# Gate products of 512 columns: the input's rounded part and remainder side by side

## The chip, the cores and the metric

The kernel runs on one core of a Trainium2 chip. The metric is the device time of one execution in microseconds (us), the median of several. A core has TensorE (PE in the profile, its weight loads PEld), VectorE (DVE), ScalarE (ACT), GpSimd (POOL), and SyncE (SP), which issues most DMAs. Each of DVE, ACT and POOL works through its instructions in the order of the program; where one engine needs another's result it waits on a semaphore.

## The reference

Two layers of a decoder trunk over 256 positions of 1024 channels. Each layer mixes tokens by three branches (latent attention A, dilated window attention B, attention over selected keys C) and then runs a mixture of 32 experts. The change concerns the gates of the branches:

```python
o_a = mla_branch(...); o_b = dilated_branch(...); o_c = dsa_branch(...)
g = jax.nn.sigmoid(x @ w_gate + b_gate).reshape(B, S, 3, D)
merged = g[:, :, 0] * (o_a @ w_a) + g[:, :, 1] * (o_b @ w_b) + g[:, :, 2] * (o_c @ w_c)
return merged @ w_o
```

`x @ w_gate` is a product of 256 × 1024 by 1024 × 3072, in float32.

## The kernel before

Float32 products of the mixer are made of three products in a faster format (fp32r). `split` (L357) cuts a float32 tile in two: ACT rounds it (L361), and DVE, at the start of a layer now and then POOL, takes the remainder (L362). `mm3` (L364) then adds rounded × rounded, rounded × remainder and remainder × rounded in PSUM (L366, L367, L368).

A layer's input, transposed, lies in two tiles of 8 × 256 columns: `xTh`, its rounded part, and `xTl`, its remainder. They are made by `make_xT` in layer 0 and by `next_T` and `next_split` in layer 1. The mixer's weights come in as a stream of DMAs into a ring of 26 slots (1 MB each). They are worked off in a fixed list of pieces, built by `pieces` (L557): first the input projection, then for each branch gates and output projections by turns, then the common output projection. A piece has `prep`, which splits 1024 columns of its weights into a slot `ws`, and `prod`, its products in two parts. `mixer` (L1326) runs part 0 and part 1 of a piece, and calls `prep` of a piece five ahead behind part 1 (four ahead near the end). After each part it pops steps of the three branches' attention from queues, by due times and estimated delays: scores, reductions (L870), exponentials (L880), division (L892), transposes (L905), products with the values (L918), top-k (L1072, L1073), the selection mask (L1082 to L1085). All that is decided when the program is built; on the chip each engine keeps to that order.

A gate piece makes one tile of 128 gate channels × 256 positions: 8 k, each with `mm3` of 256 columns, into half of a PSUM bank. There are 24 such pieces a layer, 48 in all. Behind the last product ACT runs Tanh out of the bank (L647; a sigmoid by way of tanh, its bias and scale in the instruction). `merge` (L739) multiplies the gate later with the branch's projection: L744 for branch A, L747 for B and C. PSUM has eight banks, taken in turn (`bank`). Small tiles of the tag `t1` share five buffers. `evac` (L348) copies out of PSUM on ACT or DVE, whichever has the smaller sum of estimated costs so far; `note` adds to these sums.

Of the kernel before, what the change touches and what calls it, by code (L numbers as in the profile page):

```python
# [10 lines left out]
F32 = mybir.dt.float32  # L11
F32R = mybir.dt.float32r
BF = mybir.dt.bfloat16
I32 = mybir.dt.int32
AF = mybir.ActivationFunctionType
ALU = mybir.AluOpType
# [3 lines left out]
P = 128  # L20
L = 2
T = 256
NT = 2
D = 1024
KD = 8
# [23 lines left out]
T1 = 5  # L49
# [261 lines left out]
class Trunk:  # L311
# [52 lines left out]
    def mm3(self, out, sh, sl, mh, ml, start, stop):  # L364
# [2 lines left out]
        m(out, sh, ml, start=False, stop=False)  # L367
        m(out, sl, mh, start=False, stop=stop)  # L368

    def warm(self, n, src):  # L370

        ps = self.bank()
        for _ in range(n):
            self.nc.tensor.matmul(ps, src[:, 0:P], src[:, 0:512], start=True, stop=True)
# [162 lines left out]
    def make_xT(self, t):  # L537
        nc = self.nc
        if t == 0:
            self.xTh = self.slots.alloc([P, KD, T], F32R, "xTh")  # L540
            self.xTl = self.slots.alloc([P, KD, T], F32R, "xTl")
        ts = slice(t * P, (t + 1) * P)
        for k in range(0, KD, 4):
            ps = self.bank()
            for j in range(4):
                nc.tensor.transpose(ps[:, j * P:(j + 1) * P], self.x[:, t, (k + j) * P:(k + j + 1) * P], self.ident)
            self.split(self.xTh[:, k:k + 4, ts], self.xTl[:, k:k + 4, ts], ps.rearrange("p (k t) -> p k t", k=4), 512)

    def wsplit(self, src, n, shape):
        w = self.slots.alloc([P, 2, n], F32R, "ws")  # L550
# [6 lines left out]
    def pieces(self, l):  # L557

        out = []

        def win(c):
            name, c0, w = CHUNKS[c]
            st = {}
            nk = 2 if w > 256 else 4
            np_ = KD // nk
            for i in range(np_):
                h, kk = (i // 2, i % 2) if w > 256 else (0, i)

                def prep(h=h, kk=kk):
                    raw = self.ring.get((l, "in", c, h))  # L570
                    return self.wsplit(raw[:, kk * nk:(kk + 1) * nk, :], nk * w, (P, nk, w))

                def prod(sp, part, i=i):
                    if "ps" not in st:
                        st["ps"] = [self.bank() for _ in range(NT)]
                    for t in (part,):
                        for j in range(nk):
                            k = i * nk + j
                            ts = slice(t * P, (t + 1) * P)
                            self.mm3(st["ps"][t][:, :w], self.xTh[:, k, ts], self.xTl[:, k, ts], sp[1][:, j], sp[2][:, j],  # L580
                                     k == 0, k == KD - 1)
                    if i == np_ - 1:
                        self.put_pj(st["ps"][part], part, c0, w)
                        if part:
                            self.mark(("in", c))

                last = (l, "in", c, h) if (w <= 256 and i == np_ - 1) or (w > 256 and kk == 1) else None
                out.append((prep, prod, last, None))
# [37 lines left out]
        def gates(br, q):  # L626

            for j in range(2):
                ct = q * 2 + j

                def prep(j=j):
                    raw = self.ring.get((l, "gate", br, q))
                    return self.wsplit(raw[:, :, j * P:(j + 1) * P], 1024, (P, 8, P))

                def prod(sp, part, ct=ct, st=None):
                    if part == 0:
                        self.gps = self.bank()
                    ps = self.gps
                    for k in range(part * 4, part * 4 + 4):
                        self.mm3(ps[:, :T], sp[1][:, k], sp[2][:, k], self.xTh[:, k], self.xTl[:, k], k == 0, k == KD - 1)  # L640
                    if part == 0:
                        return
                    gp = self.slots.part("g", 8)
                    g = gp.ap
                    b = br * 8 + ct
                    self.note("act", T)
                    self.nc.scalar.activation(g, ps[:, :T], AF.Tanh, bias=self.hbg[:, b:b + 1], scale=0.5)  # L647
                    self.g[br, ct] = gp
                    if br == 2 and ct == 7:
                        self.slots.free(self.xTh, self.xTl)  # L650

                out.append((prep, prod, (l, "gate", br, q) if j else None, None))

# [878 lines left out]
    def next_T(self, t):  # L1532

        nc = self.nc
        if t == 0:
            self.xTh = self.slots.alloc([P, KD, T], F32R, "xTh")
            self.xTl = self.slots.alloc([P, KD, T], F32R, "xTl")
            self.xps, self.xy = {}, {}
        xps = self.xps[t] = [self.bank() for _ in range(4)]
        for k in range(KD):  # L1540
            nc.tensor.transpose(xps[k // 2][:, k % 2 * P:(k % 2 + 1) * P], self.x[:, t, k * P:(k + 1) * P], self.ident)
# [14 lines left out]
    def next_split(self, t, h):  # L1556
        ts = slice(t * P, (t + 1) * P)
        for j in range(2):
            k = 4 * h + 2 * j
            self.split(self.xTh[:, k:k + 2, ts], self.xTl[:, k:k + 2, ts], self.xy[t, h][j], 256)  # L1560

    def ln2_out(self, t, acc, c, pool):

# [434 lines left out]
```

## Time and profile before

| | us |
|---|---|
| median of 3 runs | 982.09 (981.78 to 984.99) |
| the profiled execution | 979.94 |
| its span, first to last instruction | 978.1 |
| TensorE busy | 902.0 (92%) |
| DVE busy | 467.0 (48%) |
| ACT busy | 415.6 (42%) |
| POOL busy | 147.9 (15%) |

The first mixer takes the span up to about 290 us, the first layer's experts up to about 494, the second mixer up to about 772, the second layer's experts and the last normalisation the rest. The gates of layer 0 have their Tanh between 143.8 and about 253 us, those of layer 1 between about 626 and 736.

In the profile's timelines a row has a start, a time and an engine, then the line, the operation, the tiles (out<-in) and shapes, and the count of instructions that the row merges; brackets tell how long the engine was idle before it and what ended that. A matmul's time is longer than the distance to the next one, since matmuls overlap: its pace is read from starts.

### The profile page before, as it was taken

The numbers are of one execution on the slowest core, as the hardware profiler recorded it, in microseconds if no ns is written. First come the engines' busy times: TensorE is split into PE (matmuls) and PEld (weight loads), VectorE is DVE, ScalarE is ACT, GpSimd is POOL, SyncE is SP. The second block draws the span as 40 slices with busy tenths as digits, with TensorE's granted clock in tenths as the row PEclk, the third lists the DMA queues.
The fourth block names the chain that finished last, engine by engine and source line by source line (L and its number), as shares of the span: only waits on it lengthen the run. The fifth ranks groups of instructions, "written<-read, shape, count | busy, mean of one in ns | idle before, by whom it ended". The sixth has DMA issues, their size and how long they took to land.

```text
span 978.1 us, 18621 instructions
## 1 busy us (share of the span) xinstructions
PE 902.0 (92%) x7626; PEld 706.2 (72%) x7627; DVE 467.0 (48%) x968; ACT 415.6 (42%) x911; POOL 147.9 (15%) x246
## 2 busy tenths in 40 slices
PE   8999999999999995799889999999999999775994
PEld 7988899999995652455379888998999855441541
DVE  6848677845563110110388686677556521101104
ACT  6545556644553230222274646666345524210221
POOL 2531110012100000000035071100271000000002
PEclk9999999999999997789999999999999999986997
DMA  9933161396889999999993033415849899999993
GB/s 373 384 127 129 44 259 44 140 376 218 309 318 360 421 421 419 420 420 420 420 422 138 27 130 129 174 53 217 351 162 423 314 407 420 421 420 420 420 420 160
DMA packets 41421, 284.85 MB, mean 291 GB/s; under 512 B 4850, under 2 KB 5618, under 8 KB 9074
## 3 DMA queue, kind: packets, MB, share of 16 engines
q1 hardware_dynamic: 41044, 283.38, 72.5%
q8 instruction: 62, 1.02, 0.4%
q10 hardware_dynamic: 288, 0.23, 0.1%
q14 instruction: 27, 0.22, 0.1%
HBM read 282.55 MB, written 1.05 MB: 290 GB/s over the span
## 4 chain that ended last, share of the span: by engine, by line
PE 61%; DMA 30%; POOL 3%; DVE 2%; issue 2%; ACT 1%; SPq 0%; POOLq 0%; ACTq 0%; DVEq 0%
DMA w<-in_stream_dram 28%; PE bank L366 13%; PE bank L367 13%; PE bank L368 13%; PE bank L1730 4%; PE bank L864 3%; PE bank L1684 2%; PE bank L918 2%; PE bank L905 2%; DMA gb<-in_ln_dram 2%; PE bank L1809 2%; PE bank L867 1%; POOL t L773 1%; PE bank L485 1%; PE bank L1487 1%
## 5 line engine op out<-in xcount | busy, mean ns | idle before, releaser
L362 DVE TENSOR_TENSOR ws<-w,ws 128x1024 fp32r<-128x1024 f32 (+2 forms) x154 | 188.8, 1235 | 127.5 <-ACT ws L361 123.6
L361 ACT ACTIVATE ws<-w 128x1024 fp32r<-128x1024 f32 (+2 forms) x158 | 158.5, 1022 | 31.9 <-PE bank L368 14.4
L1730 PE MATMUL bank<-w,xg 128*32 128x256 f32 x2048 | 134.0, 401 | 31.8 <-DMA w<-in_stream_dram 24.1
L1730 PEld LDWEIGHTS bank<-w,xg 128*32 128x32 f32 x2048 | 66.5, 115 | 102.3 <-DMA w<-in_stream_dram 29.7
L366 PE MATMUL bank<-ws,xTh 128*128 128x408 f32 (+3 forms) x320 | 115.4, 361 | 1.2 <-ACT xTh L361 1.2
L366 PE MATMUL bank<-xTh,ws 128*128 128x256 f32 x384 | 111.2, 290 | 0.0
L367 PE MATMUL bank<-ws,xTh 128*128 128x408 f32 (+3 forms) x320 | 109.3, 342 | 1.2 <-POOL ws L362 1.2
L368 PE MATMUL bank<-ws,xTl 128*128 128x408 f32 (+3 forms) x320 | 109.6, 342 | 0.7 <-DVE xTl L362 0.7
L367 PE MATMUL bank<-xTl,ws 128*128 128x256 f32 x384 | 108.6, 283 | 0.0
L368 PE MATMUL bank<-xTh,ws 128*128 128x256 f32 x384 | 108.5, 283 | 0.0
L1688 ACT ACTIVATE xg<-bank,gpk 128x128 f32<-128x128 f32 x128 | 51.6, 453 | 99.6 <-PE bank L1684 96.4
L1758 DVE SCALAR_TENSOR_TENSOR t<-t,cw,bank 128x256 f32<-128x256 f32 x16 | 7.7, 480 | 156.2 <-PE bank L1730 156.2
L366 PEld LDWEIGHTS bank<-xTh,ws 128*128 128x128 f32 x384 | 73.5, 191 | 1.8 <-issue 1.0
L367 PEld LDWEIGHTS bank<-xTl,ws 128*128 128x128 f32 x384 | 73.6, 192 | 0.2
L368 PEld LDWEIGHTS bank<-xTh,ws 128*128 128x128 f32 x384 | 73.5, 191 | 0.0
L880 ACT ACTIVATE p<-bank,nb 128x128 f32<-128x128 f32 (+1 forms) x92 | 37.2, 419 | 69.9 <-DVE nb L872 62.3
L366 PEld LDWEIGHTS bank<-ws,xTh 128*128 128x128 f32 x320 | 60.5, 189 | 7.7 <-issue 1.7
L1809 PE MATMUL bank<-w,t 128*32 128x512 f32 (+1 forms) x544 | 61.8, 571 | 2.6 <-DMA w<-in_stream_dram 1.4
L368 PEld LDWEIGHTS bank<-ws,xTl 128*128 128x128 f32 x320 | 60.4, 189 | 5.3 <-DVE xTl L362 1.0
L367 PEld LDWEIGHTS bank<-ws,xTh 128*128 128x128 f32 x320 | 60.6, 189 | 4.6 <-POOL ws L362 1.5
L1684 PEld LDWEIGHTS bank<-xg,x 128*128 128x128 f32 x512 | 60.4, 192 | 3.5 <-issue 2.5
L1684 PE MATMUL bank<-xg,x 128*128 128x128 f32 x512 | 62.4, 276 | 0.0
(343 smaller groups left out, 1523.8 us busy)
## 6 DMA issues: line engine op xcount, KB each, us to landing
w<-in_stream_dram SPq DMA_DIRECT2D x252, 1024.0 KB, 13.4
w<-in_stream_dram SPq DMA_DIRECT2D x12, 816.0 KB, 14.8
w<-in_stream_dram SPq DMA_DIRECT2D x4, 832.0 KB, 8.4
w<-in_stream_dram SPq DMA_DIRECT2D x2, 768.0 KB, 12.3
x<-in_x_dram SPq DMA_DIRECT2D x2, 512.0 KB, 4.1
w<-in_stream_dram SPq DMA_DIRECT2D x2, 512.0 KB, 15.0
out_dram<-x SPq DMA_DIRECT2D x4, 256.0 KB, 2.2
masks<-in_masks_dram SPq DMA_DIRECT2D x1, 512.0 KB, 11.4
```

Of the source, the lines that this page charges most:

```text
L361: self.nc.scalar.activation(hi, src, AF.Copy)
L362: (self.nc.gpsimd if self.lo_pool else self.nc.vector).tensor_tensor(lo, src, hi.bitcast(F32), op=ALU.subtract)
L366: m(out, sh, mh, start=start, stop=False)
L367: m(out, sh, ml, start=False, stop=False)
L368: m(out, sl, mh, start=False, stop=stop)
L864: nc.tensor.matmul(b[:, j * w:(j + 1) * w], q[:, blk * P:(blk + 1) * P], k[:, 0:w], start=j == 0, stop=False)
L880: nc.scalar.activation(p[:, j], v[:, j], AF.Exp, bias=nb[:, j:j + 1], scale=u["scale"], accum_out=sm[:, j:j + 1])
L905: nc.tensor.transpose(ps[:, n * P:(n + 1) * P], p[:, j * P:(j + 1) * P], self.ident)
L1684: nc.tensor.matmul(ps[:, i * P:(i + 1) * P], self.xn[:, t, k + i], pm[:, t, j:j + Q].rearrange("p e c -> p (e c)"), start=t == 0, stop=t = ...
L1688: nc.scalar.activation(xg[:, k + i], ps[:, i * P:(i + 1) * P], AF.Identity, bias=b, scale=g)
L1730: nc.tensor.matmul(hp[i * CAP:(i + 1) * CAP, c * 256:(c + 1) * 256], xg[:, k, i * CAP:(i + 1) * CAP], w[i], start=k == 0, stop=k == KD - 1 ...
L1809: nc.tensor.matmul(yp[q * CAP:(q + 1) * CAP, :w], hT[:, j, q * CAP:(q + 1) * CAP], w2[q][:, j], start=j == 0, stop=j == 1, tile_position=( ...
```

## The change

The gates' product takes the input's rounded part and its remainder as one moving operand of 512 columns. A new `mm2` makes, for each k, one product of the rounded weights with both (512 columns, a whole bank) and one of the weights' remainder with the rounded input (256 columns, the first half). The order of the two is turned round after the first k. For that the two tiles of x are laid out anew: each of two tiles holds four k, and for each the rounded 256 columns and the 256 of the remainder side by side. Behind the last product ACT copies the second half of the bank to a `t1` tile, DVE adds the first half to it, and ACT runs Tanh on the sum. The input projection's products stay as they were, with operands from the new tiles. The estimates get one more cost on ACT and one on DVE for each gate.

```diff
+    def mm2(self, out, sh, sl, mv, start, stop):
+
+        m = self.nc.tensor.matmul
+        n = T
+        if not start:
+            m(out[:, :n], sl, mv[:, 0], start=False, stop=False)
+        m(out, sh, mv, start=start, stop=stop)
+        if start:
+            m(out[:, :n], sl, mv[:, 0], start=False, stop=False)
...
     def make_xT(self, t):
         nc = self.nc
         if t == 0:
-            self.xTh = self.slots.alloc([P, KD, T], F32R, "xTh")
-            self.xTl = self.slots.alloc([P, KD, T], F32R, "xTl")
+            self.xT = [self.slots.alloc([P, 4, 2, T], F32R, "xT") for _ in range(2)]
...
-            self.split(self.xTh[:, k:k + 4, ts], self.xTl[:, k:k + 4, ts], ps.rearrange("p (k t) -> p k t", k=4), 512)
+            self.split(*(self.xT[k // 4][:, :, j, ts] for j in range(2)), ps.rearrange("p (k t) -> p k t", k=4), 512)
...
                     for k in range(part * 4, part * 4 + 4):
-                        self.mm3(ps[:, :T], sp[1][:, k], sp[2][:, k], self.xTh[:, k], self.xTl[:, k], k == 0, k == KD - 1)
+                        self.mm2(ps, sp[1][:, k], sp[2][:, k], self.xT[k // 4][:, k % 4], k == 0, k == KD - 1)
                     if part == 0:
                         return
                     gp = self.slots.part("g", 8)
                     g = gp.ap
                     b = br * 8 + ct
                     self.note("act", T)
-                    self.nc.scalar.activation(g, ps[:, :T], AF.Tanh, bias=self.hbg[:, b:b + 1], scale=0.5)
+                    s = self.t([P, T], F32, "t1", T1)
+                    self.note("dve", T)
+                    self.note("act", T)
+                    self.nc.scalar.activation(s, ps[:, T:], AF.Copy)
+                    self.nc.vector.tensor_tensor(s, s, ps[:, :T], op=ALU.add)
+                    self.nc.scalar.activation(g, s, AF.Tanh, bias=self.hbg[:, b:b + 1], scale=0.5)
                     self.g[br, ct] = gp
...
     def next_split(self, t, h):
         ts = slice(t * P, (t + 1) * P)
         for j in range(2):
-            k = 4 * h + 2 * j
-            self.split(self.xTh[:, k:k + 2, ts], self.xTl[:, k:k + 2, ts], self.xy[t, h][j], 256)
+            self.split(*(self.xT[h][:, 2 * j:2 * j + 2, i, ts] for i in range(2)), self.xy[t, h][j], 256)
```

## Rows read from the trace of the kernel before

**Rows 1.** The page: busy time of the engines, and the chain that ended last.

```profile
PE 902.0 (92%) x7626; PEld 706.2 (72%) x7627; DVE 467.0 (48%) x968; ACT 415.6 (42%) x911; POOL 147.9 (15%) x246
...
PE 61%; DMA 30%; POOL 3%; DVE 2%; issue 2%; ACT 1%; SPq 0%; POOLq 0%; ACTq 0%; DVEq 0%
```

**Rows 2.** Busy us of each engine by stretch, granted clock, DMA share, GB/s.

```profile
136.00:150.00 14.00, 14.00 (x125) 13.57 (x124) 10.11 (x21) 9.77 (x22) 0.00 (x0) 1.00 0.25 85
150.00:170.00 20.00, 20.00 (x165) 18.43 (x164) 13.38 (x31) 11.14 (x40) 0.00 (x0) 1.00 0.14 49
170.00:190.00 20.00, 20.00 (x176) 18.65 (x176) 17.74 (x40) 11.86 (x24) 0.00 (x0) 1.00 0.44 163
...
230.00:250.00 20.00, 20.00 (x169) 20.00 (x168) 9.14 (x13) 9.46 (x15) 2.91 (x4) 1.00 0.52 183
...
318.00:445.00 127.00, 105.86 (x1110) 62.54 (x1111) 16.74 (x34) 27.55 (x69) 5.50 (x9) 0.89 1.01 420
...
660.00:680.00 20.00, 20.00 (x185) 18.08 (x184) 16.44 (x31) 11.69 (x26) 0.00 (x0) 1.00 0.54 205
```

**Rows 3.** Timeline of PE: 17 products of 512 columns, 46 of 256, first and last.

```profile
111.83 0.39 PE L367 MATMUL bank<-ws,xTh 128*128 128x512 f32 x1
...
115.49 0.39 PE L368 MATMUL bank<-ws,xTl 128*128 128x512 f32 x1
...
136.03 0.28 PE L368 MATMUL bank<-xTh,ws 128*128 128x256 f32 x1
...
141.42 0.28 PE L368 MATMUL bank<-xTh,ws 128*128 128x256 f32 x1
```

**Rows 4.** Line 647 as a whole, then ACT's timeline around gates of either layer.

```profile
L647 ACT ACTIVATE g<-bank,hbg x48: 452/473/521, 143.8 to 736.3; 128x256 f32<-128x256 f32 x48
...
136.84 0.66 ACT L352 ACTIVATE vB<-bank 128x256 f32<-128x256 f32 x2
...
143.77 0.49 ACT L647 ACTIVATE g<-bank,hbg 128x256 f32<-128x256 f32 x1
144.13 1.08 ACT L361 ACTIVATE ws<-w 128x1024 fp32r<-128x1024 f32 x1
145.08 0.49 ACT L647 ACTIVATE g<-bank,hbg 128x256 f32<-128x256 f32 x1
145.43 1.08 ACT L361 ACTIVATE ws<-w 128x1024 fp32r<-128x1024 f32 x1
...
679.55 0.47 ACT L647 ACTIVATE g<-bank,hbg 128x256 f32<-128x256 f32 x1 [1.24 <-PE bank L368]
```

**Rows 5.** DVE's timeline: the remainders of the first gates' pieces, a merge.

```profile
145.24 2.53 DVE L362 TENSOR_TENSOR ws<-w,ws 128x1024 fp32r<-128x1024 f32 x2 [2.58 <-ACT ws L361]
...
157.89 0.41 DVE L744 SCALAR_TENSOR_TENSOR merged<-g,bank 128x256 f32<-128x256 f32 x1
```

**Rows 6.** Timelines of three engines: what attention's products need, and when they run.

```profile
148.16 1.13 ACT L352 ACTIVATE qkT<-bank 128x512 f32<-128x512 f32 x2
...
153.19 0.71 PE L864 MATMUL bank<-qkT 64*128 64x128 f32 x8
...
161.00 0.23 DVE L1085 TENSOR_SCALAR cs<-cs 128x128 bf16<-128x128 f32 x1
...
162.56 0.60 PE L867 MATMUL bank<-cs,mk 128*128 128x512 bf16 x2
...
176.88 0.69 DVE L892 TENSOR_TENSOR p<-p,r 128x512 f32<-128x512 f32 x1
...
177.39 1.04 PE L905 MATMUL bank<-cst,p 128*128 128x128 f32 x8
```

**Rows 7.** PE's timeline: branch B's output is waited for, layer 0, layer 1.

```profile
205.32 0.39 PE L366 MATMUL bank<-oTB,ws 128*128 128x256 f32 x1 [0.48 <-ACT oTB L361]
...
687.30 0.39 PE L366 MATMUL bank<-oTB,ws 128*128 128x256 f32 x1 [0.48 <-ACT oTB L361]
```

**Rows 8.** Timelines: a late gate on ACT, the output projection's remainders on DVE, their use.

```profile
233.08 0.47 ACT L647 ACTIVATE g<-bank,hbg 128x256 f32<-128x256 f32 x1 [2.41 <-PE bank L368]
...
264.34 2.36 DVE L362 TENSOR_TENSOR ws<-w,ws 128x1024 fp32r<-128x1024 f32 x2 [1.44 <-ACT ws L361]
...
267.21 0.39 PE L367 MATMUL bank<-ws,mT 128*128 128x512 f32 x1
```

More of the change, by code (lines that the diff above doesn't have):

```diff
@@ L571, in prep, with prod @@
                     return self.wsplit(raw[:, kk * nk:(kk + 1) * nk, :], nk * w, (P, nk, w))
-                def prod(sp, part, i=i):
+                def prod(sp, part, n=i):
                     if "ps" not in st:
@@ L577, in prod @@
                         for j in range(nk):
-                            k = i * nk + j
+                            k = n * nk + j
                             ts = slice(t * P, (t + 1) * P)
-                            self.mm3(st["ps"][t][:, :w], self.xTh[:, k, ts], self.xTl[:, k, ts], sp[1][:, j], sp[2][:, j],
+                            self.mm3(st["ps"][t][:, :w], *(self.xT[k // 4][:, k % 4, i, ts] for i in range(2)), sp[1][:, j], sp[2][:, j],
                                      k == 0, k == KD - 1)
-                    if i == np_ - 1:
+                    if n == np_ - 1:
                         self.put_pj(st["ps"][part], part, c0, w)
@@ L646, in prod @@
                     self.note("act", T)
-                    self.nc.scalar.activation(g, ps[:, :T], AF.Tanh, bias=self.hbg[:, b:b + 1], scale=0.5)
+                    s = self.t([P, T], F32, "t1", T1)
[4 more added lines that the diff above has]
+                    self.nc.scalar.activation(g, s, AF.Tanh, bias=self.hbg[:, b:b + 1], scale=0.5)
                     self.g[br, ct] = gp
                     if br == 2 and ct == 7:
-                        self.slots.free(self.xTh, self.xTl)
+                        self.slots.free(*self.xT)
                 out.append((prep, prod, (l, "gate", br, q) if j else None, None))
@@ L1535, in next_T @@
         if t == 0:
-            self.xTh = self.slots.alloc([P, KD, T], F32R, "xTh")
-            self.xTl = self.slots.alloc([P, KD, T], F32R, "xTl")
+            self.xT = [self.slots.alloc([P, 4, 2, T], F32R, "xT") for _ in range(2)]
             self.xps, self.xy = {}, {}
```

## The prediction

> **What bounds the kernel now.** I read the page first [rows 1]: TensorE is busy 92% of the span, and the chain that ended last lies on it for 61%, on DMAs for 30%. By stage [rows 2] these are two kinds of stretch. In both mixers (the rows from 136 to 250 and from 660 us) the matmul row is full, the clock is whole and the DMA engines are 14% to 54% busy: TensorE bounds, and nothing hides time added to or taken from its queue. From 318 us the DMA engines are saturated and TensorE waits for experts' weights. All gates lie in the mixers, 24 to a layer, so what the change does there moves all that follows: the stream of experts' weights is let in by slots that the mixer frees, and moves with it.
>
> The engines beside TensorE come next. Over 230 to 250 us ACT and DVE are busy 47% and 46%; over 170 to 190 us DVE is busy 89% and ACT 59%, over 660 to 680 us 82% and 58% [rows 2]. So the two halves of the gates differ: in the first half of each layer attention runs in between, in the second it doesn't. What matters is how far ACT and DVE run behind TensorE, and what TensorE takes from them: that I read from the three engines' timelines.
>
> **TensorE's part.** For each of 8 k the change puts one product of 512 columns and one of 256 where three of 256 stood. In a gate of now, 45 products of 256 follow one another from 136.03 to 141.42 us: 0.1198 us each [rows 3]. In the input projection 16 products of 512 take from 111.83 to 115.49: 0.2288 us each [rows 3]. So a k costs 0.3594 us now and 0.3486 after: 0.0108 us saved, 0.086 a gate, 4.1 us over 48 gates × 8. The weight load that goes isn't counted by itself: it lies under the matmul before it. The two paces make a fixed 0.0108 us a product, beside 0.1090 for 256 columns. That a 256 keeps its pace between two 512s no row shows; the saving lies between none and, if it loses its fixed part too, 8 us. I take 4.1, the nearest to the rows.
>
> The Trainium skill (TensorE: Matmul & The Clock Gate, section Back-to-back issue gap) gives an isolated matmul its columns at 2.4 GHz and 2.5 ns more. By that a k saves 2.6 ns and all gates 1.0 us, and the sum below would end 1.6 us later. The trace disagrees: its 256 columns take 13 ns more than 106.7, and the trace's value stands.
>
> **ACT's and DVE's part.** Each gate now has one Tanh out of PSUM, 48 of them, 0.47 us median [rows 4]. After, ACT copies 256 columns out of PSUM, DVE adds the other half, and only then ACT runs Tanh. The copy: two of 256 columns take 0.66 us together [rows 4], 0.39 each, ACT free for the next after 0.26. The add: as DVE's merge out of PSUM, 0.41 [rows 5]. By busy time that is 48 × 0.39 = 19 us of ACT and 20 us of DVE. The price isn't in that, but in the order. Both engines take their work in the order of the code, and behind each Tanh ACT has the rounding (L361, 1.08 us) of a weight piece five ahead, behind that DVE has its remainder (L362, 1.22 us). So Tanh waits for an add, which in DVE's queue stands behind the remainder of the piece before, which waits for ACT's rounding before that. Work that overlapped becomes one chain through both engines.
>
> I walk it by hand, keeping each duration and starting each instruction when its engine and its inputs are there. Layer 0's first gate: its Tanh starts at 143.77, five us after its product (24 at 0.12 from about 135.9), so ACT is late already [rows 4]. Copy 143.77 to 144.16, add (DVE idles here) 144.19 to 144.60, Tanh at 144.63, rounding at 144.99 instead of 144.13: 0.9 us later. The second: copy at 145.94, but DVE has the first's remainder (145.24 before, now 146.10 to 147.32), so add 147.24 to 147.65, Tanh at 147.68, rounding at 148.04 instead of 145.43: 2.6 us. A gate alone costs 0.9, a gate behind a gate 1.7 more; where top-k or the softmax stands in DVE's queue too, up to 1.9 more. So through the twelve gates beside attention DVE's remainders come late by 0.9, 2.6, 4.5, 5.4, 6.2, 8.0, 9.8, 11.7, 13.0, 14.5, 16.4, 17.6 us; in layer 1, its twelve gates ending with the one at 679.55 [rows 4], by 0.9, 2.6, 3.9, 4.8, 5.6, 7.4, 9.3, 11.2, 13.0, 13.9, 15.2, 14.4.
>
> Is that under cover? TensorE's margin [rows 6]: transposed queries and keys (two copies of L352, both done at 149.29) are used from 153.19, 3.9 us; the selection mask, ready at 161.23, at 162.56, 1.3 us; probabilities, the second unit's divided until 177.57, in L905's burst of eight from 177.39, whose second half begins some 0.4 us in: 0.3 us. The margin is spent after three to five gates; from there TensorE waits. It then hands ACT and DVE time back only where these wait for TensorE, and in this stretch they seldom do. At its end TensorE already waits 0.48 us for branch B's output in either layer [rows 7], so there the lateness goes through whole: 17.5 us in layer 0, 14.3 in layer 1. What the twelve gates save on TensorE in these stretches saves nothing, since it waits.
>
> The second half: ACT waits for TensorE up to 2.41 us before a gate's Tanh [rows 8], and a gate needs 2.8 us of TensorE against 2.3 from copy to the end of rounding. These gates keep their saving: 24 × 0.086 = 2.1 us. At their end, in branch C, merges and roundings alternate; my walk ends with the remainders of the output projection's weights about 3.5 us late, and the one of the pair at 264.34 that ends at 265.57 is used at 267.21 [rows 8]: 1.6 us of margin, so 1.9 us lost in each layer.
>
> Other edits cost nothing: x's two parts in one tile take the same two slots, and are written and read by the same instructions; the accounting that picks an engine for copies gains 412 ns for ACT and 336 for DVE per gate, so a few copies may change engine.
>
> **The sum.** 17.5 + 14.3 + 2 × 1.9 − 2.1 = 33.5 us. The profiled execution took 979.94 us (span 978.1, 1.8 around it): 1013.4. The median shown is 982.09, 2.15 above that execution; I forecast 1014. The price lies between: each gate by itself, never behind another, 24 × 0.86 = 20.6, less all 4.1 saved, 996; a third of that given back by idle moments, 990; and, with both halves as walked and the clock falling (below), 1032.
>
> **Rivals.** *The look-ahead covers it.* Weights are split five pieces ahead, and over 136 to 190 us DVE has a quarter of its time free and ACT four tenths [rows 2]. Then only 4.1 us are left: 976. For it: TensorE's row is full in the gates now, and DVE's 67% over 150 to 170 us isn't a full engine [rows 2]. Against it: it decides at margins of over 15 us for transposes and masks, where [rows 6] show 0.3 to 3.9. Chance 0.09.
> *Cover in part.* TensorE's waits give enough back that a third of the toll stays, some 5 us a layer: 983 to 990. It needs ACT and DVE to idle for other causes than each other. Chance 0.08.
> *The products don't get cheaper and the copies are hidden:* no change, 979 to 985. Chance 0.04.
> *The clock.* From 318 to 445 us, where TensorE is idle 21 of 127 us, the granted clock is 0.89 [rows 2]: at the lower level, 1.2 GHz, for part of it. After the change TensorE idles some 17 of 80 us beside attention. If the clock falls once in each layer for some 10 us, up to 5 us of TensorE's work are added in each, and where ACT and DVE bound anyway less: 1016 to 1032. Single waits in my walk are 1.5 to 3.5 us long, and no row tells what waits of that length do to the clock. The Trainium skill (TensorE: Matmul & The Clock Gate, section HAM oscillation — how this bites in real kernels) has such falls come back with every wait in a loop; by that rule this rival would be the likeliest, and here a row of 0.89 under longer waits is all that bears it out. Chance 0.11.
>
> **How the numbers follow.** The forecast, a toll of 15 to 40 us from the chain through ACT and DVE, has 0.68. The range 990 to 1032 holds it and most of the clock's case and the upper edge of the part cover, some 0.8. A measurement of this kernel can tell some 0.3% from no change: faster 0.09, within 0.04, slower 0.87.
>
> **What would show it.** Right: ACT idles before each Tanh for DVE's add; TensorE is idle in front of L905, L918, L867 and L864 by about 30 us in all, nearly all of it beside attention (150 to 225 us, and the like in layer 1); the rest of the gates and the experts' stages are as long as before. The 512s show a pace of 0.23 us, the 256s 0.12. Wrong: no idle time of TensorE in the gates' stretches, a first mixer no longer than now, or idle time in front of other lines than these; a clock under 1.00 there would be the clock's case.

## The result, and the profile after

| | median of runs, us | ratio to before, 95% interval | profiled execution, us | its span, us | its granted clock |
|---|---|---|---|---|---|
| before | 981.93 | | 979.94 | 978.1 | 0.965 |
| after | 1024.65 (1022.50 to 1026.72) | 1.0446 [1.0426, 1.0467] | 1026.72 | 1025.0 | 0.958 |

The change costs 43 us. The forecast was 1014 and the range 990 to 1032: the direction and the main place are right, the size is 10.7 us too small, most of it in the second half of each layer's gates.

The page of the kernel after, its busy times and its chain of work that ended last:

```profile
PE 917.8 (90%) x7242; PEld 692.3 (68%) x7243; DVE 483.9 (47%) x1020; ACT 431.1 (42%) x955; POOL 146.9 (14%) x246
...
DMA 15%; PE 12%; DVE 5%; ACT 3%; issue 1%; POOL 0%; SPq 0%; POOLq 0%; ACTq 0%
```

Against [rows 1], DVE is busy 16.9 us more and ACT 15.5 us more, about the added copies and adds; neither is busy for half of the span. In the chain TensorE's share falls from 61% to 12% (the shares printed add up to 36% only, so this is read as a direction and no more). Which wait came up stands in the groups of instructions (line, engine, operation | busy us, mean ns of one | idle us before them and who ended it), here the gates' three:

```profile
L661 ACT ACTIVATE g<-t,hbg 128x256 f32<-128x256 f32 x48 | 24.5, 509 | 73.9 <-DVE t L660 73.9
...
L660 DVE TENSOR_TENSOR t<-t,bank 128x256 f32<-128x256 f32 x48 | 19.9, 414 | 14.5 <-ACT t L659 14.5
...
L659 ACT ACTIVATE t<-bank 128x256 f32<-128x256 f32 x48 | 18.0, 375 | 2.7 <-PE bank L376 2.6
```

ACT stands idle 73.9 us before its 48 Tanh, all of it for DVE's add. Before, it waited 28.7 us in all in front of L647, for TensorE's product.

To see where TensorE falls behind, compare the start of the same product in the two traces. First some of TensorE's rows of the kernel before that were not shown yet, where it later waits last beside attention, in layer 0 and layer 1, and at the end of layer 1's mixer:

```profile
200.83 1.09 PE L918 MATMUL bank<-p,vB 128*64 128x128 f32 x16
201.85 1.09 PE L905 MATMUL bank<-cst,pB 128*128 128x128 f32 x8
202.87 1.97 PE L918 MATMUL bank<-p,vB 128*64 128x128 f32 x32
...
682.80 1.09 PE L918 MATMUL bank<-p,vB 128*64 128x128 f32 x16
...
755.99 0.60 PE L1408 MATMUL bank<-cst,x 128*128 128x128 f32 x4
```

And TensorE's timeline of the kernel after (start, duration, and in brackets the idle time in front and who ended it):

```profile
112.60 0.39 PE L367 MATMUL bank<-ws,xT 128*128 128x512 f32 x1
...
192.63 0.68 PE L919 MATMUL bank<-cst,p 128*128 128x128 f32 x4 [3.04 <-DVE p L906]
...
217.91 2.46 PE L932 MATMUL bank<-p,vB 128*64 128x128 f32 x16 [1.64 <-ACT p L352]
220.30 1.81 PE L919 MATMUL bank<-cst,pB 128*128 128x128 f32 x8
222.04 1.42 PE L932 MATMUL bank<-p,vB 128*64 128x128 f32 x22
...
224.49 0.39 PE L366 MATMUL bank<-oTB,ws 128*128 128x256 f32 x1 [0.48 <-ACT oTB L361]
...
290.76 0.50 PE L367 MATMUL bank<-ws,mT 128*128 128x512 f32 x1 [0.77 <-DVE ws L362]
...
719.36 2.19 PE L932 MATMUL bank<-p,vB 128*64 128x128 f32 x16 [1.64 <-ACT p L352]
...
725.91 0.38 PE L366 MATMUL bank<-oTB,ws 128*128 128x256 f32 x1 [0.49 <-ACT oTB L361]
...
800.79 0.60 PE L1422 MATMUL bank<-cst,x 128*128 128x128 f32 x4
```

| place, before and after | TensorE late by, us | gained since the line above | the prediction's term |
|---|---|---|---|
| layer 0's input products, 111.83 [rows 3] and 112.60 | 0.8 | 0.8 | 0 |
| last wait beside layer 0's attention, 200.83 and 217.91 | 17.1 | 16.3 | 17.5 |
| branch B's output, 205.32 [rows 7] and 224.49 | 19.2 | 2.1 | 0 |
| output projection, 267.21 [rows 8] and 290.76 | 23.6 | 4.4 | 1.9 - 1.05 |
| layer 1, 682.80 and 719.36 (last wait) | 36.6 | 13.0 | 14.3 |
| branch B's output, 687.30 [rows 7] and 725.91 | 38.6 | 2.0 | 0 |
| end of layer 1's mixer, 755.99 and 800.79 | 44.8 | 6.2 | 1.9 - 1.05 |
| the span | 46.9 | 2.1 | 0 |

(Layer 0's experts lie inside the 13.0 and give some 0.5 us back, so the stretch beside layer 1's attention lost some 13.5.) Beside attention the loss is what was walked, less 1.2 us in layer 0 and about 0.8 in layer 1. Three things come on top: some 2 us in each layer behind the last wait, 8.9 us more than forecast in the later gates with the output projection, and 2.9 us at the two ends.

### The profile page after: what moved, and what is told of

Its sections match the earlier page's. It is cut to its first block, busy times and chain, and to the rows that moved or that the text cites. A ratio compares the mean times of both kernels' runs of the same rounds, so it can differ in the third digit from the quotient of the medians.

```text
span 1025.0 us, 17968 instructions
## 1 busy us (share of the span) xinstructions
PE 917.8 (90%) x7242; PEld 692.3 (68%) x7243; DVE 483.9 (47%) x1020; ACT 431.1 (42%) x955; POOL 146.9 (14%) x246
## 3 DMA queue, kind: packets, MB, share of 16 engines
HBM read 282.55 MB, written 1.05 MB: 277 GB/s over the span
## 5 line engine op out<-in xcount | busy, mean ns | idle before, releaser
L362 DVE TENSOR_TENSOR ws<-w,ws 128x1024 fp32r<-128x1024 f32 (+2 forms) x154 | 187.8, 1229 | 143.1 <-ACT ws L361 142.9
L361 ACT ACTIVATE ws<-w 128x1024 fp32r<-128x1024 f32 (+2 forms) x158 | 156.8, 1014 | 17.2 <-PE bank L376 5.7
L376 PE MATMUL bank<-xT,ws 128*128 128x512 f32 x384 | 138.3, 403 | 0.0
L366 PE MATMUL bank<-ws,xT 128*128 128x408 f32 (+3 forms) x320 | 115.8, 362 | 1.2 <-ACT xT L361 1.2
L368 PE MATMUL bank<-ws,xT 128*128 128x408 f32 (+3 forms) x320 | 110.1, 344 | 0.5 <-DVE xT L362 0.5
L367 PE MATMUL bank<-ws,xT 128*128 128x408 f32 (+3 forms) x320 | 109.8, 343 | 0.8 <-POOL ws L362 0.8
L375 PE MATMUL bank<-xT,ws 128*128 128x256 f32 x336 | 95.9, 285 | 0.0
L376 PEld LDWEIGHTS bank<-xT,ws 128*128 128x128 f32 x384 | 71.2, 190 | 13.0
L375 PEld LDWEIGHTS bank<-xT,ws 128*128 128x128 f32 x336 | 64.1, 191 | 3.5 <-issue 1.0
L366 PEld LDWEIGHTS bank<-ws,xT 128*128 128x128 f32 x320 | 60.7, 190 | 7.7 <-issue 1.7
L368 PEld LDWEIGHTS bank<-ws,xT 128*128 128x128 f32 x320 | 60.7, 190 | 5.1 <-DVE xT L362 0.8
L367 PEld LDWEIGHTS bank<-ws,xT 128*128 128x128 f32 x320 | 60.9, 190 | 4.1 <-POOL ws L362 1.0
L661 ACT ACTIVATE g<-t,hbg 128x256 f32<-128x256 f32 x48 | 24.5, 509 | 73.9 <-DVE t L660 73.9
L1767 ACT ACTIVATE t<-bank 128x256 f32<-128x256 f32 x16 | 6.1, 383 | 95.9 <-PE bank L1742 95.9
## 6 DMA issues: line engine op xcount, KB each, us to landing
w<-in_stream_dram SPq DMA_DIRECT2D x2, 512.0 KB, 15.9
```

Source lines behind the costliest of these rows:

```text
L361: self.nc.scalar.activation(hi, src, AF.Copy)
L362: (self.nc.gpsimd if self.lo_pool else self.nc.vector).tensor_tensor(lo, src, hi.bitcast(F32), op=ALU.subtract)
L366: m(out, sh, mh, start=start, stop=False)
L375: m(out[:, :n], sl, mv[:, 0], start=False, stop=False)
L376: m(out, sh, mv, start=start, stop=stop)
```

## Experiments

One kernel each; the differences are against the changed kernel unless said otherwise. The kernel before ran beside them: 980.84 to 981.14 us.

**1. The products alone.**

```diff
-                    self.nc.scalar.activation(s, ps[:, T:], AF.Copy)
-                    self.nc.vector.tensor_tensor(s, s, ps[:, :T], op=ALU.add)
-                    self.nc.scalar.activation(g, s, AF.Tanh, ...)
+                    self.nc.scalar.activation(g, ps[:, :T], AF.Tanh, ...)
```

> The new products and the new layout of the input alone: Copy and add are left out and the Tanh reads the first half of the bank, so the product of the rounded weights with the input's remainder never reaches the gate (that part of the computation is left out). Theory 1 (the chain of Copy, add and Tanh behind each gate's last product costs the time): all of the loss goes, and the 48 gates keep the saving of some 0.09 us each that the later gates showed, 4 us, so 976 to 980 us; if the first 0.8 us of lateness and the last 2.4 us belong to the layout, 979 to 983. Theory 3 (the 512-column products or the interleaved layout are slower): above 1000.

Measured: 978.55 us, ratio 0.9967 [0.9953, 0.9981]. The new products and the new layout of x cost nothing; they bring 2.6 us by the medians (1.9 to 4.6 by the interval); 48 gates at 0.086 would give 4.1. The kernel leaves out one of the gate's three products, so it is a test and not a version for use.

**2. The chain alone.**

```diff
-                        self.mm2(ps, sp[1][:, k], sp[2][:, k], self.xT[k // 4][:, k % 4], ...)
+                        x = self.xT[k // 4][:, k % 4]
+                        self.mm3(ps[:, :T], sp[1][:, k], sp[2][:, k], x[:, 0], x[:, 1], ...)
...
-                    self.nc.scalar.activation(s, ps[:, T:], AF.Copy)
+                    self.nc.scalar.activation(s, ps[:, :T], AF.Copy)
...
-                    self.nc.scalar.activation(g, s, AF.Tanh, ..., scale=0.5)
+                    self.nc.scalar.activation(g, s, AF.Tanh, ..., scale=0.25)
```

> The chain alone: the three products of before on 256 columns, then Copy out of the bank, an add of the bank to the copy, and the Tanh with half the scale, so the result is the same. Theory 1 (the chain): all of the loss and none of the saving, 1026 to 1031 us. Theory 3 (products or layout): 978 to 986.

Measured: 1026.27 us, ratio 1.0454 [1.0437, 1.0472]. With 1 and 2 the change falls apart cleanly: all of the loss is in Copy, add and Tanh, the small gain in the products.

**3. The same work with no hand-over.** Products of before, Tanh straight from the bank, and

```diff
+                    ja, jd = (self.t([P, T], F32, "t1", T1) for _ in range(2))
+                    self.nc.scalar.activation(ja, self.cst[:, 0:T], AF.Copy)
+                    self.nc.vector.tensor_tensor(jd, self.cst[:, 0:T], self.cst[:, 0:T], op=ALU.add)
```

> The work without the chain: the three products of before, the Tanh straight from the bank, and for each gate one Copy on ACT and one add on DVE from a constant, which nobody waits for. ACT and DVE are as busy as in the changed kernel, but no instruction of theirs stands waiting for the other. Theory 1 (it is the waiting in the chain, with the pieces' splits queued behind it): 982 to 994 us. Theory 2 (it is the added busy time of ACT and DVE, 48 times about 0.9 us in sum): 1010 or more.

Measured: 995.01 us, ratio 1.0133 [1.0116, 1.0150]: a third of the loss, between the two answers. The groups of instructions of this run name what I had overlooked: the two tiles come from a set of five ("t1") that is shared by rope, the step on GpSimd that turns queries and keys by their positions, and rope now waits for them.

```profile
L662 ACT ACTIVATE g<-bank,hbg 128x256 f32<-128x256 f32 x48 | 22.9, 477 | 15.2 <-PE bank L368 15.2
...
L788 POOL TENSOR_TENSOR t<-cqT,cst 128x128 f32<-128x128 f32 x6 | 4.8, 804 | 65.4 <-ACT t L660 33.0 <-DVE ws L362 25.4 <-PE bank L1065 6.9
```

Tanh waits for TensorE alone, 15.2 us; rope's wait for `t` (33.0 us in this row) is not there in the kernel before, where the same row waits 48.2 us in all. TensorE pays for it: it waits 3.2 us in layer 0 and 4.3 us in layer 1 for rope's result, which it doesn't before, and with each of these waits the granted clock falls to 0.50, for 3.4 and 6.8 us. So the trace puts most of the 14 us down to rope's wait; no run takes it out by itself. The changed kernel takes such a tile too.

**4. The same work, in other tiles.** As 3, but

```diff
-                    self.nc.scalar.activation(ja, self.cst[:, 0:T], AF.Copy)
-                    self.nc.vector.tensor_tensor(jd, self.cst[:, 0:T], self.cst[:, 0:T], op=ALU.add)
+                    self.nc.scalar.activation(g, self.cst[:, 0:T], AF.Copy)
+                    self.nc.vector.tensor_tensor(ps[:, T:], self.cst[:, 0:T], self.cst[:, 0:T], op=ALU.add)
```

> The run with the added Copy and add that nobody waits for, once more, but they write into the gate's own tile and into the free half of the gate's bank instead of two of the shared small tiles. That run lost 14 us. Theory 5 (its loss was rope on GpSimd waiting for the shared tiles): 980 to 985 us. Theory 2 (busy time of ACT and DVE): 990 to 997 again.

Measured: 1025.86 us, ratio 1.0469 [1.0451, 1.0486]: the whole loss, against both expectations. The groups say why: the add that was meant to be nobody's now stands in front of Tanh.

```profile
L661 ACT ACTIVATE g<-bank,hbg 128x256 f32<-128x256 f32 x48 | 22.7, 474 | 68.2 <-DVE bank L660 67.5
```

Tanh reads one half of the bank, the add writes the other, and still Tanh waits for it (67.5 us over the 48 gates): in this program the two are kept in order. Rope's long wait is gone here (48.2 us for its six pieces, as before) and the loss is back. So as a test of busy time this run failed, but it shows something better: Tanh needs no data from the Copy or the add for the loss to come; it is enough that it stands behind an add in DVE's queue. That it is the add's turn in the queue and not its 0.41 us, run 5 says.

**5. Tanh behind the next piece's split.** ACT rounds the piece ahead while DVE adds:

```diff
-                    self.nc.scalar.activation(g, s, AF.Tanh, ...)
+                    self.tanh.append(lambda: self.nc.scalar.activation(g, s, AF.Tanh, ...))
...
                         prep(i + j)
+                    while self.tanh:
+                        self.tanh.pop(0)()
```

> The whole change, but the Tanh of a gate is issued only after the splits of the piece ahead, so that ACT does that piece's rounding while DVE adds. Theory 1 (the chain holds up the splits): at least half of the 43 us comes back, 984 to 1004 us. Theory 2 (busy time) and theory 3 (products): nothing comes back, 1018 to 1030.

Measured: 987.44 us, ratio 1.0058 [1.0041, 1.0075]. Three instructions of the same kind and length for each gate, and 37 of the 43 us are back. Of the 6 us that are left a part is rope's: TensorE waits 3.0 and 3.8 us for it, once in each layer.

**6 and 7. The gate's own tile** for Copy and add (`s = g` in place of a tile of "t1"): alone, and together with the late Tanh.

> The whole change, but Copy and add write into the gate's own tile instead of one of the five small tiles that rope, the merges and others share. In the changed kernel GpSimd's rope waits 16.8 us for the first gate's Tanh because of that tile. Theory 1 (the chain of ACT and DVE costs the time and covers this wait): no more than 4 us better than the change, 1019 to 1026 us. Theory 5 (the shared tiles are the larger part): 1005 to 1015 or less.

Measured: 1025.26 us, ratio 1.0452 [1.0434, 1.0470]: nothing gained. Rope's wait is real in the changed kernel, but lies under the chain.

> The Tanh issued behind the splits of the piece ahead and the gate's own tile, both. With the late Tanh alone the run was 6 us above the kernel before, and nearly all of that is lost once in each layer, at the wait for rope's result beside the first gates. If that wait comes from the shared tile, 975 to 981 us, at or below the kernel before. If it comes from the chain, 984 to 989 as with the late Tanh alone.

Measured: 984.42 us, ratio 1.0040 [1.0026, 1.0055]: 3 us better than with the late Tanh alone (the two intervals just overlap), and TensorE's waits for rope are gone. So the tile does cost where the chain is opened, but the gate's own tile doesn't bring the 975 to 981 expected. ACT's and DVE's timelines of this run at layer 0's first two gates:

```profile
144.68 0.40 ACT L660 ACTIVATE g<-bank 128x256 f32<-128x256 f32 x1
144.94 1.08 ACT L362 ACTIVATE ws<-w 128x1024 fp32r<-128x1024 f32 x1
145.89 0.53 ACT L662 ACTIVATE g<-g,hbg 128x256 f32<-128x256 f32 x1
146.29 0.40 ACT L660 ACTIVATE g<-bank 128x256 f32<-128x256 f32 x1
146.55 1.08 ACT L362 ACTIVATE ws<-w 128x1024 fp32r<-128x1024 f32 x1
147.64 0.51 ACT L662 ACTIVATE g<-g,hbg 128x256 f32<-128x256 f32 x1
...
145.10 0.42 DVE L661 TENSOR_TENSOR g<-g,bank 128x256 f32<-128x256 f32 x1 [1.54 <-ACT g L660]
146.05 1.23 DVE L363 TENSOR_TENSOR ws<-w,ws 128x1024 fp32r<-128x1024 f32 x1 [0.53 <-ACT ws L362]
```

The rounding (L362 here) starts behind the Copy, and Tanh finds its sum ready. The next gate's rounding comes 1.61 us behind the first's (144.94, 146.55); in the changed kernel 3.08 us (145.31, 148.39).

**8 and 9. One half of each layer at a time.** `mm2`, Copy and add in the first twelve gates of a layer alone (beside attention), or in the last twelve alone; the others take `mm3` and the direct Tanh.

```diff
+                    new = br * 8 + ct < 12        # or: >= 12
...
+                        if new:
                             self.mm2(...)
+                        else:
+                            self.mm3(ps[:, :T], ...)
```

> The change in the first twelve gates of each layer alone (beside attention); the other twelve keep the three products of before and the direct Tanh. In the changed kernel TensorE lost 18.4 and 15.7 us in these two stretches. Theory 1 (the loss is made there by the chain): those 34 us and the 0.8 at the start, 1012 to 1019 us. Rival (a later loss depends on an earlier one, or the clock carries it): outside of that.

Measured: 1013.97 us, ratio 1.0343 [1.0323, 1.0362]: 33.1 us lost.

> The change in the last twelve gates of each layer alone. The prediction gave them 2 x 1.9 us less 2.1 saved: with 0.8 at the start 982 to 985 us. Theory 1 by the trace of the changed kernel (ACT and DVE go round in one closed loop there, 3.08 us a gate where TensorE needs 2.8): 5.4 and 7.0 us lost less some 1.8 saved, 988 to 994 us, with the first half as before.

Measured: 989.93 us, ratio 1.0103 [1.0083, 1.0124], 9.1 us, where the prediction had 1.7. The two add up to 42.2 of the 43 us: the halves hardly depend on each other, and most of the missing part of the forecast lies in the second.

**10. Two more adds** in the last twelve gates of each layer:

```diff
-                        self.nc.vector.tensor_tensor(s, s, ps[:, :T], op=ALU.add)
+                        for op in (ALU.add, ALU.subtract, ALU.add):
+                            self.nc.vector.tensor_tensor(s, s, ps[:, :T], op=op)
```

> The change in the last twelve gates of each layer alone, with DVE adding, subtracting and adding the bank again: two more operations of 0.41 us for each of these gates, the result the same but for rounding. The run with one add took 990 us. Theory 1 (one loop through ACT and DVE sets the pace here, so each instruction in it counts in full): 24 x 0.82 = 20 us more, 1004 to 1012. By the prediction's own reckoning (2.3 us of chain a gate against TensorE's 2.8) a gate would now need 3.1 and lose 0.3: 6 to 8 us more, 995 to 999.

Measured: 1009.96 us, ratio 1.0308 [1.0291, 1.0325]: 20.0 us above run 9. DVE's timeline in branch C, two gates behind one another:

```profile
254.67 1.22 DVE L362 TENSOR_TENSOR ws<-w,ws 128x1024 fp32r<-128x1024 f32 x1 [1.53 <-ACT ws L361]
255.81 1.32 DVE L667 TENSOR_TENSOR t<-t,bank 128x256 f32<-128x256 f32 x3
258.66 1.23 DVE L362 TENSOR_TENSOR ws<-w,ws 128x1024 fp32r<-128x1024 f32 x1 [1.53 <-ACT ws L361]
```

From remainder to remainder it is 3.99 us here and 3.08 with one add (267.51 and 270.59 in the changed kernel): three adds take 1.32 us where one takes 0.41, and the round is longer by just that 0.91. For 24 gates that makes 21.8 us, of which 20.0 show in the time: nearly the full length of what was put into the loop.

**11. Everything still later.** With the gate's own tile, the add behind the remainder of the piece ahead, and Tanh behind the step of attention that follows:

```diff
-                    self.nc.vector.tensor_tensor(s, s, ps[:, :T], op=ALU.add)
+                    self.adds.append(lambda: self.nc.vector.tensor_tensor(s, s, ps[:, :T], op=ALU.add))
...
                         prep(i + j)
+                    while self.adds:
+                        self.adds.pop(0)()
                 debt = self.run_fg(self.rate(i + 0.5 * part) / 2 + debt)
+                while part and self.tanh:
+                    self.tanh.pop(0)()
```

> All gates with the new products and the gate's own tile; the add now behind DVE's remainder of the piece ahead, and the Tanh behind the attention step that follows. In the run with the late Tanh alone moved DVE still waited 5.9 us for the Copy and ACT 5.8 us for the add beside layer 0's attention, and 3 us of lateness came from there. Theory 1: without these waits nearly all of the saving of 4 us is left, 976 to 981 us. Rival: the later Tanh holds up the attention's own steps on ACT, 983 to 990.

Measured: 1010.42 us, ratio 1.0308 [1.0290, 1.0325], worse than either expectation. The add now stands behind the remainder of the rounding that was just issued, and Tanh ahead of the next rounding: the loop is closed again, one place further on. ACT waits before Tanh nearly as long as in the changed kernel (73.9 us there):

```profile
L662 ACT ACTIVATE g<-g,hbg 128x256 f32<-128x256 f32 x48 | 24.5, 510 | 72.6 <-DVE g L661 72.6
```

Later is not better; by runs 5 and 11 together, what counts is that Tanh's add stands behind an *older* remainder than that of the rounding ACT does in the meantime.

**12. A version for use:** the change in the last twelve gates of each layer, with the late Tanh and the gate's own tile.

> The change in the last twelve gates of each layer alone, with the late Tanh and the gate's own tile. With the Tanh right behind the add these twelve cost 9 us. Theory 1 (a loop of ACT and DVE, opened by the late Tanh): the loss goes and 24 x 0.086 us are saved, 977 to 981 us. Rival (the new products themselves or the merges keep part of the loss): 983 or more.

Measured: 978.89 us, ratio 0.9979 [0.9969, 0.9988], 2.1 us below the kernel before, as much as 24 × 0.086. It beats the kernel before by some 0.2%, and the changed kernel by 4.5%.

## Why the prediction came out as it did

**The mechanism: right.** Work that overlapped becomes one chain through ACT and DVE. Runs 1 and 2 put all of the loss into it, and run 5 takes most of it back by order alone. ACT's and DVE's timelines after, at the first two gates, to be read beside [rows 4, 5]:

```profile
143.95 0.39 ACT L659 ACTIVATE t<-bank 128x256 f32<-128x256 f32 x1
144.90 0.51 ACT L661 ACTIVATE g<-t,hbg 128x256 f32<-128x256 f32 x1 [0.56 <-DVE t L660]
145.31 1.04 ACT L361 ACTIVATE ws<-w 128x1024 fp32r<-128x1024 f32 x1
146.26 0.36 ACT L659 ACTIVATE t<-bank 128x256 f32<-128x256 f32 x1
147.98 0.51 ACT L661 ACTIVATE g<-t,hbg 128x256 f32<-128x256 f32 x1 [1.36 <-DVE t L660]
148.39 1.04 ACT L361 ACTIVATE ws<-w 128x1024 fp32r<-128x1024 f32 x1
...
146.39 1.23 DVE L362 TENSOR_TENSOR ws<-w,ws 128x1024 fp32r<-128x1024 f32 x1 [1.53 <-ACT ws L361]
147.53 0.41 DVE L660 TENSOR_TENSOR t<-t,bank 128x256 f32<-128x256 f32 x1
```

The walk had the first rounding at 144.99 and the second at 148.04; they start at 145.31 and 148.39, 0.3 us later, of which 0.2 are the first Copy's (143.95 for 143.77). The copy takes 0.375 us for 0.39, the add 0.414 for 0.41.

**The products: right.** TensorE's timeline after, in a gate:

```profile
137.26 0.28 PE L375 MATMUL bank<-xT,ws 128*128 128x256 f32 x1
...
139.00 0.28 PE L375 MATMUL bank<-xT,ws 128*128 128x256 f32 x1
```

Five k, each of one product of 256 columns and one of 512, take from 137.26 to 139.00: 0.348 us each, where the prediction had 0.3486. So a 256 does keep its pace between two 512s.

**The stretches beside attention: right in size, with more in it than was said.** 17.5 and 14.3 us against 16.3 and, without the half microsecond that the experts give back, some 13.5. The half measured by itself gives 33.1 (run 8) for 31.8. TensorE waits where it was said: 3.04 us before L919 (before: L905) for DVE's probabilities, 1.64 before L932 (L918). But its idle time before the four lines named comes to some 19 us and not 30. It also waits 2.0 and 2.7 us for rope, in front of a line that wasn't named, and it lost time at a lower clock (below).

**The later gates: the term that was mis-sized.** The prediction set TensorE's 2.8 us a gate against "2.3 from copy to the end of rounding", let these gates keep their saving, and put the loss at the end of each layer at 1.9 us. But 2.3 is the way from one Copy to the end of one rounding and not the period. The period goes on through DVE's remainder, because the next add stands behind it: the same thing that the walk beside attention had counted ("a gate behind a gate"); its own roundings, at 144.99 and 148.04, are 3.05 us apart. ACT's and DVE's timelines after, in branch C:

```profile
266.02 0.51 ACT L661 ACTIVATE g<-t,hbg 128x256 f32<-128x256 f32 x1 [1.35 <-DVE t L660]
266.43 1.04 ACT L361 ACTIVATE ws<-w 128x1024 fp32r<-128x1024 f32 x1
...
269.10 0.51 ACT L661 ACTIVATE g<-t,hbg 128x256 f32<-128x256 f32 x1 [1.36 <-DVE t L660]
269.51 1.05 ACT L361 ACTIVATE ws<-w 128x1024 fp32r<-128x1024 f32 x1
...
276.42 0.51 ACT L661 ACTIVATE g<-t,hbg 128x256 f32<-128x256 f32 x1 [1.36 <-DVE t L660]
...
267.51 1.23 DVE L362 TENSOR_TENSOR ws<-w,ws 128x1024 fp32r<-128x1024 f32 x1 [1.52 <-ACT ws L361]
268.65 0.41 DVE L660 TENSOR_TENSOR t<-t,bank 128x256 f32<-128x256 f32 x1
```

Round once: rounding 266.43, remainder 267.51, add 268.65, Tanh 269.10, rounding 269.51. That is 3.08 us a gate, more than TensorE's 2.8. With an output piece between, Tanh at 266.02 is followed by the one at 276.42 two gates and one piece later: 10.4 us. TensorE has less than that to do (16 k of 0.35 us for two gates, 24 products of 0.12 for the piece: 8.5), so here too the two engines set the pace, and the lead of five pieces is used up until TensorE waits: 0.77 us before L367 at 290.76. Run 9 gives 9.1 us for this half where the prediction's sum had 1.7, and run 10 shows the price of the loop by making it 0.91 us longer: 20.0 us. Run 12 opens the loop in these same gates, and the loss is gone. This is 7.4 of the 10.7 us by which the forecast was short.

**The clock: a rival that came in beside the forecast.** Granted clock by stretch, kernel after (us, busy us of PE, PEld, DVE, ACT, POOL, clock, DMA share, GB/s):

```profile
136.00:163.00 27.00, 23.68 (x158) 19.50 (x157) 15.29 (x33) 16.33 (x46) 2.37 (x4) 1.00 0.17 63
163.00:190.00 27.00, 23.33 (x157) 20.10 (x155) 17.82 (x44) 12.88 (x39) 0.00 (x0) 1.00 0.33 117
...
194.52:197.91 3.39, 3.39 (x19) 2.65 (x19) 3.35 (x7) 0.00 (x0) 0.00 (x0) 0.50 0.00 0
218.42:221.81 3.39, 3.39 (x21) 3.06 (x22) 1.84 (x4) 2.44 (x6) 0.00 (x0) 0.50 0.63 198
```

Two stretches in each layer's mixer at 0.50, the lower level (1.2 GHz), where both mixers of before stand at 1.00 (in part [rows 2]); the other two lie at 696.28 and 720.17. The first of each pair was followed by another wait of TensorE, which could take up what was lost. The second wasn't: from 217.91 the 16 products of L932 and 8 of L919 take 4.13 us (to 222.04), where the same 24 took 2.04 us before (200.83 to 202.87), and TensorE, 17.08 us late ahead of them, is 19.17 late behind them. The same in layer 1: 36.56 and 38.61. Half of 3.39 us is 1.7, so of these 2.1 us a layer up to 1.7 are the clock's in this execution, some 3.4 in all; the rest stays open. No run holds the clock up, but the runs differ in it. In runs 1, 7, 9 and 12 it is 1.00 throughout both mixers; here the gates' stretches of run 9:

```profile
136.00:260.00 124.00, 122.60 (x971) 111.52 (x970) 79.54 (x150) 69.46 (x153) 9.70 (x12) 1.00 0.52 197
620.00:760.00 140.00, 135.17 (x1022) 120.00 (x1021) 87.87 (x153) 76.33 (x167) 25.68 (x24) 1.00 0.58 216
```

So run 9's 9.1 us, and with them the mis-sized term, owe nothing to falls of the clock in the mixers, by its profiled execution. In run 8 the clock is 0.50 for 20.4 us in five stretches, so up to 10.2 of its 33.1 could be the clock's; waits that follow may cover them. In run 5 it is 10.2 us, so the clock may have a part in the 3 us between runs 5 and 7. The Trainium skill (TensorE: Matmul & The Clock Gate, section HAM oscillation — how this bites in real kernels) has the clock fall again in every turn of a loop whose waits are of some 3 to 5 us, longer than most waits of the prediction's walk (1.5 to 3.5). The trace bears that out in part: a wait of 3.04 us and even one of 1.64 were each followed by a fall; the stretches 136 to 190, with 7 us of idle time among them, stay at 1.00.

**The ends.** 0.8 us of the profiled execution are lost before layer 0's first product of 512 columns. It isn't the layout: run 8, with the same layout, starts the product that stands at 111.83 before and 112.60 after at 111.87.

```profile
111.87 0.39 PE L367 MATMUL bank<-ws,xT 128*128 128x512 f32 x1
```

Its cause stays open, as does that of the last 2.1 us, behind layer 1's mixer; the profiled execution is itself 2.1 us above the median.

**The range: partly luck.** Its upper end, 1032, was to be the walk with the clock falling. But 1014 and twice the 5 us that the clock was given make 1024, and 1024.65 was measured. With the end that its own terms give, the range would have just missed.

**What the prediction didn't list.** "x's two parts ... Other edits cost nothing" left out that Copy and add take a tile of the set that rope, merges and latents share. GpSimd's rope waits 16.8 us for it in layer 0 and 15.9 in layer 1. In the changed kernel that wait costs nothing (run 6); with the chain opened it costs some 3 us (runs 5 and 7).

**Busy time alone.** Run 7 carries all of the added work of ACT and DVE and lies 5.9 us above run 1, which carries none; it still has waits, 18.0 us of ACT for the add. So the work itself is worth some 6 us at most of the 46 between run 1 and the changed kernel.

## What to carry to other kernels

When a step on one engine is replaced by a hand-over to another engine and back, don't price its instructions but follow both queues once round: if the second engine's turn stands behind work that waits for the first, the period is the sum of everything in that loop, and where the loop is slower than the consumer, an operation put into it counts at nearly its full length (run 10). A look-ahead covers lateness that comes once; a loop slower than the consumer uses up any lead. The cure is order, not speed: issue the step that needs the answer behind the work that doesn't, so that each engine has something older to do; and give the intermediate its own tile.

## What the hardware showed that was not expected

In the changed kernel the granted clock was 0.50 for 3.4 us behind a wait of 3.04 us, which ended 12 us in which TensorE was idle for 5.6, and again behind a wait of 1.64 us that came after 14 us of nearly full work (202 to 216 us, idle 0.5); a wait of 1.99 us before 147.98 was followed by no fall. The forecast had only a row of 0.89 under longer waits. And a read of one half of a PSUM bank stood behind another engine's write to its other half (run 4: 67.5 us of waiting); whether the chip asks for that order or only the program's own waits, the run doesn't tell.
